# Encoder layer with PEER experts, one core: two builds' transposes stand ahead of blocks of U, and the loop's first G is loaded in the middle of the last build

## The chip, the cores and the metric

The kernel runs on one core of a Trainium2 chip. The metric is the device time of one execution in microseconds (us). The time before is the median of three runs, 1491.64 us (1488.11 to 1492.6). The profile shows one execution of its own, and durations are taken from that one.

Engine names: PE does the matrix products (PEld loads its weights), DVE the elementwise work on vectors, ACT the activations and copies, POOL issues the indirect DMAs (gathers), SP issues most plain DMAs; ACT issues DMAs too, in its own instruction stream.

## The reference

One encoder layer over 512 tokens of width 1024. The last part is the one that matters here:

```
h   = LN1(alpha * h + concat(a_na, a_mla) @ W_o)
q   = h @ w_q                        # 8 heads, two halves of 128
v1,i1 = top16(q[:half] @ sub_keys[0]);  v2,i2 = top16(q[half:] @ sub_keys[1])
cv,ci = top16(v1[:,None] + v2[None,:])          # 16 of 16384 experts per head
e1,e2 = i1[ci // 16], i2[ci % 16];  idx = e1 * 128 + e2;  g = softmax(cv)
ffn = sum_e  g_e * gelu(h . u_table[idx_e]) * v_table[idx_e]      # 128 experts per token
h   = LN2(alpha * h + ffn + sigmoid(h @ W_g + b_g) * (p @ W_ple))
```

## The kernel before

The 512 tokens are four chunks of 128. For chunk 0 the experts' rows are gathered from DRAM (POOL) and reduced on DVE. For chunks 1 to 3 the experts are computed densely: for each of 128 blocks of 128 experts, `ge = gelu(U_block . h)`, times a weight matrix `G` (tokens by experts, mostly zero), times the block of V. For chunk 1 (`NGC`) the 128 own rows of U are gathered too (`own_rows`), and their result stands in `G` in place of the softmax weight, so for this chunk `ge` is not needed.

Before the dense loop, `G` is built, one chunk at a time: first chunk 2, then chunk 3, then chunk 1. They are called chunk 2's, chunk 3's and the last build below. `build_g` starts with three transposes on PE (`tr` from e1, e2 and the weights, L1090), from which DVE and ACT make `eT` (L1098 to L1104). Then come 16 steps `q` of eight tokens: DVE and ACT write one-hots (`oh_i`, `oh_j`, L1144 to L1156), PE multiplies them 16 times into `tr` (L1115), ACT copies that to a staging tile `g_st` (L1128). Each four steps fill one staging tile, of which `send` writes four parts to DRAM, one per call; `send` is an instruction of ACT. Two tiles are used in turn, so the third group of a build waits for the writes of the first. The last two groups of the last build stay on the chip. The loop's first eight rows of G come from one load, `first_g` (tile `gt1`, L1447), of the two earlier builds' share; the last build copies its own share in on ACT (L1132).

PE has other work to put in between: the products of blocks of U with chunks 2 and 3, called blocks below (`lead_block`, L1291, eight products each, tiles `mm` and `hp`). 108 of the 128 blocks are done before the loop. Their loads (`raw`, `raw_u`, and at first borrowed tiles) are issued by SP as tiles come free, at most four in the ring.

The order on each engine is written by hand: the code runs inside `tc.manual_schedule`, so what is written first stands first. `run_pe(amount)` emits blocks of U on PE until a planned debt `due` is paid; `run(steps, share)` walks a build's steps and lets `own` (the gathers and reductions of rows on DVE) take a share beside them. After the own rows of chunk 1, `beside()` does the first 26 gathered rows of chunk 0 in the same way, and cuts two blocks of V near its end.

Every DMA that SP or ACT issues takes one of eight semaphores in turn, and waits for the transfer that used it last.

Of the kernel before, what the change touches and what calls it, by code (L numbers as in the profile page):

```python
# [9 lines left out]
F32 = mybir.dt.float32  # L10
# [21 lines left out]
N_S = 128  # L32
N_U = N_D - N_S
GT = 32
G_PARTS = 4
GB = 8
LEAD = 108
SPILL = 96
# [2 lines left out]
FIRST = 40  # L41
PACE = 1.1
AHEAD = 14.0
LAG = 6.0
BESIDE = 26
PRE = BESIDE
OWN = 1.2
OWN_G = 0.7
OWN_G_LATE = 4.0
SEAM = 7.0  # L50
WAIT = 8.4
OWN_LATE = 10.0
LATE = 0.57
OT = 8
# [25 lines left out]
def tile_encoder_layer(ctx: ExitStack, tc: tile.TileContext, A: dict, out: bass.AP):  # L80
    nc = tc.nc
# [8 lines left out]
    dram = ctx.enter_context(tc.tile_pool(name="dram", bufs=1, space=bass.MemoryType.DRAM))  # L90
# [205 lines left out]
    with tc.tile_pool(name="ln0", bufs=1, reuse_waits="tile") as ln0, \  # L296
# [122 lines left out]
        parts = turn(0)  # L419
# [17 lines left out]
        parts = turn(1)  # L437
# [8 lines left out]
        parts = turn(2)  # L446
# [8 lines left out]
        parts = turn(3)  # L455
# [374 lines left out]
    NGC, NDC = N_G // 128, N_D // 128  # L830
    NTG = N_D // GT
    u_rows, v_rows = A["u_rows"], A["v_rows"]
    ge_dram = dram.tile([SPILL, 128, N_U], F32, name="ge_dram")
    g_dram = dram.tile([NTG, 128, 128 * GT], F32, name="g_dram")

    pB = ctx.enter_context(tc.tile_pool(name="pB", bufs=1, reuse_waits="tile"))
    base = [pB.tile([128, D], F32, name=f"base_{c}") if c < NGC else h[c] for c in range(4)]
# [104 lines left out]
    for g in range(16):  # L942
# [8 lines left out]
        if g:  # L951
            i, t = next(homes)
# [113 lines left out]
    parts = []  # L1066

    def send():

        if parts:  # L1070
            g, t, x = parts.pop(0)
            n = 128 // G_PARTS
            nc.scalar.dma_start(g_dram[g][:, x * n * GT:(x + 1) * n * GT],
                                t[:, x * n:(x + 1) * n].rearrange("p i t -> p (i t)"))

    def run_pe(amount):
        nonlocal due
        due += amount * PACE
        while due > 0:
            done = next(pe_work, 1e9)  # L1080
            due -= done
        if due < -1e6:
            due = 0.0

    def build_g(c, e1, e2, gw):

        nonlocal due, nst
        ps = ps_tile("tr")
        for i, x in enumerate((e1, e2, gw)):
            nc.tensor.transpose(ps[:, i * 128:(i + 1) * 128], x, ident)  # L1090
        due -= 0.35
        yield None
        e32 = bt.tile([128, 3, 128], F32, name="eT", bufs=1)
        ne = e32[:, 2]
        eT = e32[:, 0:2].rearrange("p a b -> p (a b)").bitcast(F16).rearrange("p (x g s t) -> p x g s t", x=2, s=2, t=OT)
        keys, wt = eT[:, 0], eT[:, 1]
        pairs = bt.tile([128, 128, 2], F16, name="ne", bufs=1)
        nc.vector.tensor_copy(keys.rearrange("p g s t -> p s g t"),  # L1098
                              ps[:, 0:256].rearrange("p (s g t) -> p s g t", s=2, t=OT))
        w = ps[:, 256:384].rearrange("p (g t) -> p g t", t=OT)  # L1100
        nc.scalar.mul(wt[:, :, 0], w, W_SCALE)
        nc.scalar.mul(ne, ps[:, 0:128], -1.0)
        nc.vector.tensor_copy(pairs, iota.unsqueeze(2).to_broadcast([128, 128, 2]))
        nc.vector.scalar_tensor_tensor(wt[:, :, 1], w, W_SCALE, wt[:, :, 0], op0=OP.mult, op1=OP.subtract)  # L1104
        yield 1.2
        np_ = OT // 2

        def products(q, oh, oj):
            out = []
            for r in range(OT // 4):  # L1110
                ps = ps_tile("tr")
                for i in range(4):
                    a, b = divmod(4 * r + i, 2)
                    for part in range(2):
                        nc.tensor.matmul(ps[:, i * 128:(i + 1) * 128], oj[:, part, a, :, b], oh[:, a, :, b],  # L1115
                                         start=(part == 0), stop=(part == 1))
                out.append(ps)
            return out

        def leave(q, sums):  # L1120
            nonlocal stage, nst
            if q * OT % GT == 0:
                gone(f"bs{nst % 2}")
                stage = bs[nst % 2].tile([128, 128, GT], F32, name="g_st")
                nst += 1
            for r, ps in enumerate(sums):
                x = OT * q % GT + 4 * r
                nc.scalar.mul(stage[:, :, x:x + 4], ps.rearrange("p (t i) -> p i t", t=4), 1.0 / W_SCALE)  # L1128
            if (q + 1) * OT % GT == 0:
                g = (c - NGC) * (128 // GT) + q * OT // GT  # L1130
                if c == NGC:
                    nc.scalar.copy(first_g[:, g], stage[:, SPILL:SPILL + GB, :])  # L1132
                if c == NGC and g >= N_S // GT - 2:
                    g_last.append(stage)
                else:
                    parts.extend((g, stage, x) for x in range(G_PARTS))

        stage = None
        ahead = None
        wide = [128, 2 * np_, 128, 2]  # L1140
        for q in range(128 // OT):
            oh = bt.tile(wide, F16, name="oh_i")
            by_v = [128, 2 * np_ - OI_ACT, 128, 2]
            nc.vector.tensor_tensor(oh[:, OI_ACT:], pairs.unsqueeze(1).to_broadcast(by_v),  # L1144
                                    keys[:, q].rearrange("p s (a b) -> p (s a) b", b=2)[:, OI_ACT:].unsqueeze(2)
                                    .to_broadcast(by_v), op=OP.is_equal)
            for i in range(2 * OI_ACT):
                nc.scalar.activation(oh[:, i // 2, :, i % 2], iota, AF.Abs, bias=ne[:, OT * q + i:OT * q + i + 1])
            nc.scalar.activation(oh[:, 0:OI_ACT], oh[:, 0:OI_ACT], AF.Relu, bias=1.0, scale=-1.0)
            if ahead:  # L1150
                sums = products(*ahead)
                due -= G_SPLIT
            yield SPLIT_OH
            oj = bt.tile([128, 2, np_, 128, 2], F16, name="oh_j")
            for part in range(2):
                nc.vector.tensor_tensor(oj[:, part], oh[:, np_:],  # L1156
                                        wt[:, q, part].rearrange("p (a b) -> p a b", b=2).unsqueeze(2)
                                        .to_broadcast([128, np_, 128, 2]), op=OP.mult)
                if part == 0:
                    yield SPLIT_OJ  # L1160
            if ahead:
                leave(ahead[0], sums)
            ahead = (q, oh, oj)
            yield SPLIT_OJ
        sums = products(*ahead)
        due -= G_SPLIT
        yield 0.3
        leave(ahead[0], sums)
# [250 lines left out]
    with tc.manual_schedule(engines={nc.vector.engine, nc.scalar.engine, nc.tensor.engine, nc.sync.engine,  # L1419
                                     nc.gpsimd.engine}):  # L1420
        fill()
        held = []
        run(route(NGC, held))
        own = own_rows(*held)
        run_pe(next(own))
        own_due = -OWN_LATE
        for c in range(NGC + 1, 4):
            res = []
            if c > NGC + 1:
                run(route(0, []), OWN)  # L1430
            run(route(c, res), OWN)
            if c > NGC + 1:
                run_pe(WAIT)
            run(build_g(c, *res), OWN)
        own_due = 1e9
        run([0.0], 1.0)
        side = beside()
        run_pe(next(side))
        for _ in own:
            pass  # L1440
        own = None
        run_pe(LAG)

        while parts:
            send()
        first_g = pX.tile([128, NTG, GB, GT], F32, name="gt1")
        nc.sync.dma_start(first_g[:, 128 // GT:].rearrange("p g i t -> p g (i t)"),  # L1447
                          g_dram[128 // GT:, :, SPILL * GT:(SPILL + GB) * GT].rearrange("g p x -> p g x"))
        build = build_g(NGC, *held)
        next(build)  # L1450
        run_pe(next(side))
        own = side
        own_due = -OWN_G_LATE
        run(build, OWN_G)
        for x in own:
            run_pe(x)
        while parts:
            send()
        pb.close()
# [3 lines left out]
    def load_g(n, q, t, opens):  # L1463

        i = order[n]
        if opens:
            if n // GB % 2 == 0:
                t = pX.tile([128, NTG, GB, GT], F32, name="gt1")
            else:
                t = pV.tile([128, NTG, GB, GT], F32, name="gt0")  # L1470
        g = slice(q * NTG // 4 + (q == 1), (q + 1) * NTG // 4 - (q == 0))
        if q < 2:
            nc.scalar.copy(t[:, N_S // GT - 2 + q], g_last[q][:, i:i + GB, :])
        nc.sync.dma_start(t[:, g].rearrange("p g i t -> p g (i t)"),
                          g_dram[g, :, i * GT:(i + GB) * GT].rearrange("g p x -> p g x"))
        return t

    def block_of_u(n):
# [84 lines left out]
    with tc.manual_schedule(engines={nc.vector.engine, nc.sync.engine}):  # L1563
        for n, i in enumerate(order):
# [38 lines left out]
            parts = [t.rearrange("p (g t) -> p g t", t=GT) for t in (ah, al)] + [a]  # L1603
            if n in v_cut:
                held_a.append([t[:, :N_S // GT] for t in parts])
                parts = [t[:, N_S // GT:] for t in parts]
# [131 lines left out]
```

## Time and profile before

| what | value |
|---|---|
| median of three runs | 1491.64 us |
| profiled execution, its own time | 1489.54 us |
| its span, first to last instruction | 1487.8 us |
| PE busy in the span | 1450.2 us, 97% |
| DVE busy | 1268.5 us, 85% |
| chunk 3's build | 712 to 803 us |
| last build | 803 to 880 us |
| dense loop on PE | 893 to 1477 us |

Times in views are from the span's start. A timeline row has start, duration, engine, line and operation; in brackets stands the idle time before it and what ended that. "x16" is a number of records; an f32 product of the program (blocks of U) leaves two records, an f16 one leaves one.

### The profile page before, as it was taken

The numbers are of one execution on the slowest core, as the hardware profiler recorded it, in microseconds if no ns is written. First come the engines' busy times: TensorE is split into PE (matmuls) and PEld (weight loads), VectorE is DVE, ScalarE is ACT, GpSimd is POOL, SyncE is SP. The second block draws the span as 40 slices with busy tenths as digits, with TensorE's granted clock in tenths as the row PEclk, the third lists the DMA queues.
The fourth block names the chain that finished last, engine by engine and source line by source line (L and its number), as shares of the span: only waits on it lengthen the run. The fifth ranks groups of instructions, "written<-read, shape, count | busy, mean of one in ns | idle before, by whom it ended". The sixth has DMA issues, their size and how long they took to land.

```text
span 1487.8 us, 22518 instructions
## 1 busy us (share of the span) xinstructions
PE 1450.2 (97%) x7693; PEld 1212.4 (81%) x7693; DVE 1268.5 (85%) x2736; ACT 638.4 (43%) x1203; POOL 570.7 (38%) x520
## 2 busy tenths in 40 slices
PE   9999999999999999999998999999999999999997
PEld 5788777788888878888887888988888888888775
DVE  7376786579998979998776987999899999999997
ACT  3355776243221554212555763444343333333433
POOL 1013110010014544344442435665555666666630
PEclk9999999999999999999999999999999999999999
DMA  7333340175239999999999999999999999999992
GB/s 255 99 111 92 97 128 30 29 245 170 100 125 351 334 416 415 405 324 336 392 416 410 376 396 369 415 417 417 401 393 411 412 412 411 412 412 412 411 362 85
DMA packets 196851, 453.82 MB, mean 305 GB/s; under 512 B 18945, under 2 KB 96897, under 8 KB 196738
## 3 DMA queue, kind: packets, MB, share of 16 engines
q1 hardware_dynamic: 119168, 211.72, 38.6%
q0 software_dynamic: 57984, 207.12, 35.5%
q10 hardware_dynamic: 19586, 33.57, 5.9%
q8 instruction: 60, 0.98, 0.2%
q14 instruction: 53, 0.43, 0.1%
HBM read 411.70 MB, written 37.75 MB: 302 GB/s over the span
## 4 chain that ended last, share of the span: by engine, by line
PE 56%; DMA 22%; DVE 9%; issue 6%; ACT 4%; POOL 3%; SPq 0%; ACTq 0%; DVEq 0%; POOLq 0%
PE acc L1551 16%; DMA raw<-in_v_rows_dram 11%; PE mm L1291 6%; PE hp L1291 5%; DMA ge_dram<-ge 4%; PE mm L129 4%; PE mm L131 4%; PE mm L130 4%; PE pj L129 3%; PE pj L130 3%; PE pj L131 3%; DMA v_raw<-in_v_rows_dram 3%; PE hp L129 1%; PE hp L131 1%; PE hp L130 1%
## 5 line engine op out<-in xcount | busy, mean ns | idle before, releaser
L110 DVE TENSOR_TENSOR wlo<-raw,whi 128x1024 fp32r<-128x1024 f32 (+4 forms) x113 | 131.5, 1164 | 45.7 <-ACT whi L110 45.4
L110 ACT CAST a_hi<-gt 128x384 fp32r<-128x384 f32 (+2 forms) x128 | 64.9, 509 | 242.4 <-DVE gt L1598 179.5
L110 ACT CAST whi<-raw 128x1024 fp32r<-128x1024 f32 (+4 forms) x113 | 113.0, 1001 | 106.9 <-PE mm L130 47.3
L1291 PE MATMUL mm<-whole,raw 128*128 128x256 f32 x672 | 153.1, 381 | 1.5 <-DMA raw<-in_uT_dram 1.5
L1174 POOL DMA_INDIRECT whi<-in_u_rows_dram,s_ix x51 | 64.2, 1259 | 218.5 <-DVE cand L994 129.7
L1551 PE MATMUL acc<-hTh,a_hi 128*128 128x512 f32 x456 | 141.8, 391 | 0.1
L1551 PE MATMUL acc<-hTl,a_hi 128*128 128x512 f32 x456 | 141.2, 390 | 0.0
L1551 PE MATMUL acc<-hTh,a_lo 128*128 128x512 f32 x456 | 140.9, 389 | 0.0
L1291 PEld LDWEIGHTS mm<-whole,raw 128*128 128x128 f32 x672 | 125.6, 190 | 17.9 <-DMA raw<-in_uT_dram 1.9
L1534 POOL DMA_INDIRECT gat<-in_v_rows_dram,i_sel x64 | 100.8, 1574 | 55.0 <-DVE base L1536 39.5
L110 ACT CAST hTh<-v_raw 128x1024 fp32r<-128x1024 f32 x74 | 77.8, 1051 | 55.9 <-PE acc L1551 23.1
L1551 PEld LDWEIGHTS acc<-hTl,a_hi 128*128 128x128 f32 x456 | 85.4, 188 | 18.3 <-DVE hTl L110 0.4
L1551 PEld LDWEIGHTS acc<-hTh,a_lo 128*128 128x128 f32 x456 | 85.4, 188 | 18.2 <-DVE a_lo L110 0.3
L1551 PEld LDWEIGHTS acc<-hTh,a_hi 128*128 128x128 f32 x456 | 84.1, 188 | 17.2 <-ACT a_hi L110 1.1
L110 DVE TENSOR_TENSOR hTl<-v_raw,hTh 128x1024 fp32r<-128x1024 f32 x74 | 90.2, 1219 | 6.4 <-ACT hTh L110 6.4
L1551 PE MATMUL acc<-wlo,a_hi 128*128 128x512 f32 x300 | 92.8, 390 | 0.2
L1551 PE MATMUL acc<-whi,a_hi 128*128 128x512 f32 x300 | 92.8, 391 | 0.1
L1551 PE MATMUL acc<-whi,a_lo 128*128 128x512 f32 x300 | 92.6, 390 | 0.0
L1174 POOL DMA_INDIRECT wlo<-in_u_rows_dram,s_ix x51 | 61.9, 1213 | 68.3 <-DVE s_dot L1176 56.0
L1519 POOL DMA_INDIRECT gat<-in_u_rows_dram,i_sel x52 | 69.1, 1329 | 45.2 <-DVE hdot L1525 34.1
L1536 DVE SCALAR_TENSOR_TENSOR base<-gat,hdot,base 128x1024 f32<-128x1024 f32 x64 | 82.0, 1281 | 1.0
L1273 ACT ACTIVATE ge<-mm 128x256 f32<-128x256 f32 x78 | 29.6, 380 | 110.4 <-PE mm L1291 100.5
(415 smaller groups left out, 3815.7 us busy)
## 6 DMA issues: line engine op xcount, KB each, us to landing
raw<-in_uT_dram SPq DMA_DIRECT2D x80, 512.0 KB, 7.8
v_raw<-in_v_rows_dram SPq DMA_DIRECT2D x78, 512.0 KB, 13.2
raw<-in_v_rows_dram SPq DMA_DIRECT2D x48, 512.0 KB, 13.8
g_dram<-g_st ACTq DMA_DIRECT2D x40, 512.0 KB, 12.1
ge_dram<-ge ACTq DMA_DIRECT2D x96, 128.0 KB, 7.0
ge<-ge_dram SPq DMA_DIRECT2D x96, 128.0 KB, 13.0
gt<-g_dram SPq DMA_DIRECT2D x30, 384.0 KB, 13.9
raw_u<-in_uT_dram SPq DMA_DIRECT2D x19, 512.0 KB, 7.8
```

Of the source, the lines that this page charges most:

```text
L110: cut = nc.scalar.copy(hi, src), nc.vector.tensor_tensor(lo, src, r32(hi), op=OP.subtract)
L129: nc.tensor.matmul(ps, a[0], b[0], start=start, stop=False)
L130: nc.tensor.matmul(ps, a[0], b[1], start=False, stop=False)
L131: nc.tensor.matmul(ps, a[1], b[0], start=False, stop=stop)
L1174: nc.gpsimd.indirect_dma_start(out=u[:], out_offset=None, in_=u_rows, in_offset=bass.IndirectOffsetOnAxis(ap=ix[:, k:k + 1], axis=0))
L1273: nc.scalar.activation(ge, ps[:, :N_U], AF.Gelu)
L1291: nc.tensor.matmul(ps[:, :N_U], raw[:, k], whole[:, k, :], start=(k == 0), stop=(k == 7))
L1519: nc.gpsimd.indirect_dma_start(out=u[:], out_offset=None, in_=u_rows, in_offset=bass.IndirectOffsetOnAxis(ap=i_sel[:, c, k:k + 1], axis=0))
L1534: nc.gpsimd.indirect_dma_start(out=u[:], out_offset=None, in_=v_rows, in_offset=bass.IndirectOffsetOnAxis(ap=i_sel[:, c, k:k + 1], axis=0))
L1536: nc.vector.scalar_tensor_tensor(base[c], u, hdot[:, c, k:k + 1], base[c], op0=OP.mult, op1=OP.add)
L1551: nc.tensor.matmul(acc[c][hf], a[:, cs], b[:, hf * 512:(hf + 1) * 512], start=(n == 0 and i == 0), stop=(n == 127 and i == 2))
```

## The change

Four edits:

1. `WAIT` 8.4 to 3.0 and `LAG` 6.0 to 1.0: fewer blocks of U are emitted ahead of the transposes of chunk 3's build and of the last build.
2. After the last build's transposes, `GAP_ROWS` = 4 gathered rows of chunk 0 stand on DVE before the build goes on, where one stood.
3. The three last parts of chunk 3's G are no longer sent in one go ahead of the last build; the sends go on one by one. `first_g` is loaded when step q = 6 of the last build is written.
4. The last build's first two groups are written to a DRAM tensor of their own, `g_own`.

```diff
-LAG = 6.0
+LAG = 1.0
-WAIT = 8.4
+WAIT = 3.0
+FIRST_G_AT = 6
+GAP_ROWS = 4
...
-    g_dram = dram.tile([NTG, 128, 128 * GT], F32, name="g_dram")
+    g_own = dram.tile([N_S // GT - 2, 128, 128 * GT], F32, name="g_own")
+    g_dram = dram.tile([NTG - N_S // GT, 128, 128 * GT], F32, name="g_dram")
...
-            nc.scalar.dma_start(g_dram[g][:, x * n * GT:(x + 1) * n * GT],
+            to = g_own[g] if g < N_S // GT else g_dram[g - N_S // GT]
+            nc.scalar.dma_start(to[:, x * n * GT:(x + 1) * n * GT],
...
+    def load_first():
+        while parts and parts[0][0] >= N_S // GT:
+            send()
+        nc.sync.dma_start(first_g[:, N_S // GT:].rearrange("p g i t -> p g (i t)"),
+                          g_dram[:, :, SPILL * GT:(SPILL + GB) * GT].rearrange("g p x -> p g x"))
...
+            if c == NGC and q == FIRST_G_AT:
+                load_first()
...
         run_pe(LAG)
-        while parts:
-            send()
         first_g = pX.tile([128, NTG, GB, GT], F32, name="gt1")
-        nc.sync.dma_start(first_g[:, 128 // GT:].rearrange("p g i t -> p g (i t)"),
-                          g_dram[128 // GT:, :, SPILL * GT:(SPILL + GB) * GT].rearrange("g p x -> p g x"))
         build = build_g(NGC, *held)
         next(build)
-        run_pe(next(side))
+        for _ in range(GAP_ROWS):
+            run_pe(next(side))
         own = side
```

How instructions move. On PE, at the start of chunk 3's build, the order before is (`tr<-ident` are the transposes, the last row the build's first product):

```order
L1291 MATMUL mm<-whole,raw 128x256 x24
L1090 MATMUL tr<-ident,e_6432 128x128
L1090 MATMUL tr<-ident,e_6599 128x128
L1090 MATMUL tr<-ident,gw 128x128
L1291 MATMUL mm<-whole,raw_u 128x256 x8
L1291 MATMUL mm<-whole,raw 128x256 x18
L1115 LDWEIGHTS oh_j
L1115 MATMUL tr<-oh_i,oh_j 128x128
```

and with the change, at the same place:

```order
L1304 MATMUL mm<-whole,raw 128x256 x10
L1101 MATMUL tr<-ident,e_6433 128x128
L1101 MATMUL tr<-ident,e_6600 128x128
L1101 MATMUL tr<-ident,gw 128x128
L1304 MATMUL mm<-whole,raw 128x256 x14
L1304 MATMUL mm<-whole,raw_u 128x256 x8
L1304 MATMUL mm<-whole,raw 128x256 x4
L1126 LDWEIGHTS oh_j
```

14 products of blocks of U moved from ahead of the transposes to later places; between the transposes and the first product 26 stand in both.

On PE, at the start of the last build (behind the last product of the build before it), the order before is:

```order
L1291 MATMUL mm<-whole,raw_u 128x256 x4
L1291 MATMUL mm<-whole,raw 128x256 x13
L1090 MATMUL tr<-ident,e1s 128x128
L1090 MATMUL tr<-ident,e2s 128x128
L1090 MATMUL tr<-ident,gws 128x128
L1291 MATMUL mm<-whole,raw 128x256 x11
L1115 LDWEIGHTS oh_j
```

and with the change:

```order
L1304 MATMUL mm<-whole,raw 128x256 x4
L1101 MATMUL tr<-ident,e1s 128x128
L1101 MATMUL tr<-ident,e2s 128x128
L1101 MATMUL tr<-ident,gws 128x128
L1304 MATMUL mm<-whole,raw 128x256 x5
L1304 MATMUL mm<-whole,raw_u 128x256 x8
L1304 MATMUL mm<-whole,raw 128x256 x6
L1126 LDWEIGHTS oh_j
```

Ahead of the transposes 17 products became 4, behind them 11 became 19. What is left over goes to the end: behind the last build's last product and ahead of the loop's first `acc` stand 50 products of blocks of U instead of 33.

On ACT, at the same place, the order before is (the DMA rows are the sends of G and of `ge`):

```order
L1273 ACTIVATE ge<-mm 128x256
L1275 DMA ge_dram<-ge 128x256
L1073 DMA g_dram<-g_st 128x1024 x3
L1101 ACTIVATE eT<-tr 128x16x8
L1102 ACTIVATE eT<-tr 128x128
L1148 ACTIVATE oh_i<-iota,eT 128x128 x4
L1149 ACTIVATE oh_i<-oh_i 128x512
```

and with the change:

```order
L1286 ACTIVATE ge<-mm 128x256
L1288 DMA ge_dram<-ge 128x256
L1112 ACTIVATE eT<-tr 128x16x8
L1113 ACTIVATE eT<-tr 128x128
L1077 DMA g_dram<-g_st 128x1024
L1159 ACTIVATE oh_i<-iota,eT 128x128 x4
L1160 ACTIVATE oh_i<-oh_i 128x512
L1077 DMA g_dram<-g_st 128x1024 x2
```

The three sends moved from ahead of `eT` to behind it, one ahead of the first one-hot and two behind it. On SP the load of `first_g` (`gt<-g_dram`, 128x8x256) moved back past four loads of blocks of U, with fewer loads left between it and the loads of V. On DVE three more gathered rows (`row`, `whi`, `wlo`) stand ahead of `eT`; the first cut of a block of V (`hTl<-gb`) stands ahead of the last step's `oh_j` instead of behind it, and so does ACT's half of it ahead of the last copies to `g_st`.

More of the change, by code (lines that the diff above doesn't have):

```diff
@@ L1474, in load_g @@
         nc.sync.dma_start(t[:, g].rearrange("p g i t -> p g (i t)"),
-                          g_dram[g, :, i * GT:(i + GB) * GT].rearrange("g p x -> p g x"))
+                          (g_dram[g.start - N_S // GT:g.stop - N_S // GT] if q else g_own)
+                          [:, :, i * GT:(i + GB) * GT].rearrange("g p x -> p g x"))
         return t
```

## The prediction

> **What bounds the kernel now.** I read the busy times of the page first, then windows of the stages that the change touches, then who waited for whom, then the timeline at the two places where transposes stand.
>
> ```profile
> PE 1450.2 (97%) x7693; PEld 1212.4 (81%) x7693; DVE 1268.5 (85%) x2736; ACT 638.4 (43%) x1203; POOL 570.7 (38%) x520
> ```
>
> PE is busy 97% of the span, and the change adds and removes no product. So it can gain only idle time of PE, and it can lose only by new idle time. The next rows are windows: length, busy us of PE, PEld, DVE, ACT and POOL, then the granted clock, the DMA share and GB/s. They are chunk 3's build, the last build with the blocks behind it, the loop, and ten us inside the last build.
>
> ```profile
> 700.00:803.00 103.00, 99.82 (x646) 87.55 (x645) 79.97 (x132) 55.79 (x138) 45.63 (x39) 1.00 1.02 407
> 803.00:893.30 90.30, 84.62 (x571) 74.07 (x569) 70.59 (x113) 59.62 (x148) 28.49 (x24) 0.98 0.99 389
> 893.30:1443.00 549.70, 549.37 (x2641) 461.82 (x2640) 522.49 (x700) 213.73 (x307) 333.03 (x226) 1.00 1.03 407
> 860.00:870.00 10.00, 8.28 (x60) 7.28 (x58) 9.96 (x15) 8.65 (x23) 4.38 (x4) 0.83 1.03 418
> ```
>
> PE is idle 3.18 us in chunk 3's build, 5.68 in the last one, 0.33 in the loop. So what is at stake is 8.9 us, 0.6% of the time. The waits of PE (total, times, longest) say for what, the first two rows in chunk 3's build, the other four in the last:
>
> ```profile
> PE tr L1115 <- ACT g_st L1128: 2.3, 3, 1.5
> PE tr L1115 <- DVE oh_j L1156: 0.9, 1, 0.9
> ...
> PE tr L1115 <- ACT g_st L1128: 2.8, 2, 1.7
> PE mm L1291 <- DMA raw<-in_uT_dram: 1.5, 1, 1.5
> PE tr L1115 <- ACT oh_i L1149: 1.1, 1, 1.1
> PE tr L1115 <- DVE oh_j L1156: 0.3, 1, 0.3
> ```
>
> PE waits for ACT and DVE, though DVE itself stands still at the start of both builds. The timeline:
>
> ```profile
> 701.43 10.52 PE L1291 MATMUL mm<-whole,raw 128*128 128x256 f32 x48
> 711.79 0.38 PE L1090 MATMUL tr<-ident,e 128*128 128x128 f32 x2
> 712.32 0.42 DVE L1098 CAST eT<-tr 128x256 f16<-128x256 f32 x1 [5.90 <-PE tr L1090]
> ...
> 800.94 1.22 DVE L1176 CUSTOM_DVE_ANT_0 wlo<-wlo,h 128x1024 f32<-128x1024 f32 x1
> 802.36 1.94 PE L1291 MATMUL mm<-whole,raw_u 128*128 128x256 f32 x8
> 804.14 5.78 PE L1291 MATMUL mm<-whole,raw 128*128 128x256 f32 x26
> 809.97 0.27 PE L1090 MATMUL tr<-ident,gws 128*128 128x128 f32 x1
> 810.35 0.42 DVE L1098 CAST eT<-tr 128x256 f16<-128x256 f32 x1 [8.18 <-PE tr L1090]
> 811.29 2.24 ACTq L1073 DMA_DIRECT2D g_dram<-g_st  x3
> 813.58 0.28 ACT L1101 ACTIVATE eT<-tr 128x128 f16<-128x128 f32 x1 [5.41 <-DMA ge_dram<-ge]
> 814.06 0.29 DVE L1104 SCALAR_TENSOR_TENSOR eT<-tr,eT 128x128 f16<-128x128 f32 x1 [3.09 <-ACT eT L1102]
> 816.08 0.22 PE L1115 MATMUL tr<-oh_i,oh_j 128*128 128x128 f16 x1 [1.09 <-ACT oh_i L1149]
> ```
>
> The transposes stand behind blocks of U, and DVE loses 5.90 us in the one build and 8.18 + 3.09 in the other; the 3.09 are ACT's, which makes its half of `eT` only after three sends of G.
>
> **The change part by part.** The sum is made against the profiled execution, 1489.54 us with a span of 1487.8; that is 2.1 us under the median of the runs, 1491.64, and the same difference is taken off the median.
>
> *Chunk 3's transposes.* 48 records are 24 products and take 10.36 us to the next start, 0.432 each. 14 of them less put the transposes 6.0 us earlier, which takes away DVE's 5.90. PE reaches the first product 6.0 us earlier too, since 26 products stand behind the transposes as before. So PE, DVE and ACT run this build in the same relation, some 6 us earlier; no gain yet, since the 14 products are only owed. Its 3.18 us of idle I keep: the sends and the DMA rate that hold ACT are the same. Ends: all 3.2 gained, or as much lost again.
>
> *Last build's start.* Its transposes now stand 4 products (1.7 us) behind 802.36, so at 804.2 on the old scale. DVE first does three more rows, whose gathers POOL issued here; the median from issue to landing between 740 and 803 us is in the next rows:
>
> ```profile
> 793.32 1.16 POOL L1174 DMA_INDIRECT row<-in_u_rows_dram,i_sel  x1 [5.37 <-DVE s_dot L1176]
> 796.25 1.03 POOL L1174 DMA_INDIRECT wlo<-in_u_rows_dram,i_sel  x1 [0.30 <-issue]
> ...
> g_dram<-g_st ACTq DMA_DIRECT2D x12, 512.0 KB, 14.2
> raw<-in_uT_dram SPq DMA_DIRECT2D x10, 512.0 KB, 7.7
> wlo<-in_u_rows_dram,s_ix POOLq DMA_INDIRECT x6, 12.6
> row<-in_u_rows_dram,s_ix POOLq DMA_INDIRECT x4, 11.2
> ```
>
> The rows land at 804.5 to 808.9, so DVE ends the third at about 809 to 810 and reads the transposes hardly earlier than at 810.35. It has done 3 x 1.22 = 3.7 us of rows by then, and ACT's sends no longer stand ahead of `eT` (3.1): DVE is about 7 us ahead of its old place, on top of the 6. PE comes to its first product after 4 + 19 products, at 802.4 + 9.9 + 0.5 = 812.8; DVE needs 0.3 + 0.95 + 1.3 us behind `eT`, so 812.5 to 813.5. The old wait of 1.39 shrinks to about 0.4: **gain 1.0** (ends: 1.4 gained; 3 lost, if a send held ACT as long as before, 3.09).
>
> *The load of first_g.* SP sat on it for 11.5 us, until chunk 3's last part of G was written, and PE then missed a block of U:
>
> ```profile
> SPq L1447 <- DMA g_dram<-g_st: 11.5, 1, 11.5
> ...
> 827.99 1.56 PE L1291 MATMUL mm<-whole,raw 128*128 128x256 f32 x6 [1.46 <-DMA raw<-in_uT_dram]
> ```
>
> At q = 6, some 22 us into the 16 steps (814 to 873 us, rows above and below), those writes, 14.2 us long, have landed, and the writes of the last build go to `g_own`, for which the load doesn't wait. In the queue it stands between loads of U for blocks not yet due. **Gain 1.4** (0 to 1.46).
>
> *The middle of the last build.* The remaining two gaps, 1.11 and 1.72, and a product group slow at a granted clock of 0.83 (window 860 to 870 above):
>
> ```profile
> 853.59 1.09 ACT L1128 ACTIVATE g_st<-tr 128x512 f32<-128x512 f32 x2 [2.09 <-DMA g_dram<-g_st]
> 855.94 1.08 PE L1115 MATMUL tr<-oh_i,oh_j 128*128 128x128 f16 x16
> 859.04 1.11 PE L1115 MATMUL tr<-oh_i,oh_j 128*128 128x128 f16 x16 [1.11 <-ACT g_st L1128]
> 861.87 1.86 PE L1115 MATMUL tr<-oh_i,oh_j 128*128 128x128 f16 x16 [1.72 <-ACT g_st L1128]
> ```
>
> 16 products took 1.86 us instead of 1.08, so these two gaps cost 2.83 + 0.78 = 3.6. ACT was late because the third staging tile waited 2.09 us for the writes of the first. Those writes keep their length, and an earlier DVE doesn't shorten them: I take a third, **gain 1.2** (0 to 3.6). By the Trainium skill, page "TensorE: Matmul & The Clock Gate", section "Why this matters for your kernels", the array falls back only after a gap of some 3 us; the trace disagrees with that bound, with 1.72 and the slow group behind it, and by the page alone the ceiling of this term would be 2.8.
>
> *Costs put at nothing.* ACT's and DVE's halves of the first cut of V now stand inside the build's end, about 1.2 us each. DVE had its last `oh_j` done 3.7 us before PE used it and is now further ahead:
>
> ```profile
> 873.29 1.28 DVE L1156 TENSOR_TENSOR oh_j<-oh_i,eT 128x1024 f16<-128x1024 f16 x2
> 878.27 1.08 PE L1115 MATMUL tr<-oh_i,oh_j 128*128 128x128 f16 x16
> 886.58 7.07 PE L1291 MATMUL hp<-whole,raw 128*128 128x256 f32 x32
> ```
>
> The 17 products owed (7.3 us) stand ahead of the loop; they are no new work. Their four or five loads need 7.7 us each with four tiles in the ring, and a block takes 8 x 0.432 = 3.5 us, so the ring covers 13.8; without that cover a late load costs up to 4 us once. The loop's own order is unchanged, apart from `g_own`'s name.
>
> Sum: 1.0 + 1.4 + 1.2 = 3.6 us earlier at the loop's first `acc`, which was at 893.3. In the loop PE is idle 0.33 us in 550, so I let the end move as far: 1489.5 becomes 1485.9, the median 1491.6 becomes **1488.0**.
>
> **The rivals.**
>
> *All idle goes.* DVE and ACT come so early that the gaps of both builds vanish: 3.2 + 5.7 + 0.8 = 9.7 us at most, and half of chunk 3's and all of the last build's is 8: 1482 to 1486. For it: nearly all gaps are waits for ACT or DVE, which gain 13 us of lead, while PE gives up 7.3 of its own. Against it: ACT's waits on writes of G.
>
> *The loop eats it.* The loop runs at 407 GB/s with a DMA share of 1.03, and no row shown is above 418; DVE is busy 522 of 550. If its DMA stream is the true limit, PE starts earlier and later waits for V, and the end stays: 1491.6, give or take 1.5. Against it: PE kept its full pace with 0.33 us of idle, and the same transfers start earlier as well. The Trainium skill, page "DMA: Bandwidth & Descriptors", section "Where 436 GB/s comes from", puts the ceiling of the ports at 435; the trace's 407 to 418 lie near it, which speaks for this rival.
>
> *Slower: ACT's sends wait for their semaphores.* Now a send stands between `eT` and the first one-hot, and two behind it. Each waits for the transfer that had its semaphore before, which takes up to 14.2 us from issue by the row of G's writes. ACT may be late by about 1 us before PE is; beyond that PE waits one for one. To end 4.5 us above, the waits must come to 3.6 + 4.5 + 1 = 9 us: 1496 to 1500. Against it: the same three sends cost ACT 5.41 together before.
>
> **How the numbers follow.** Changes under 0.3%, 4.5 us, can't be told from none here. Chances: partial gain 0.40 (1485.5 to 1490, of which 0.14 lies beyond 4.5 us), all idle gone 0.24, eaten by the loop 0.22, slower 0.14. So faster 0.24 + 0.14 = 0.38, within 0.3% 0.26 + 0.22 = 0.48, slower 0.14. The likeliest case's own range is 1485.5 to 1490; the range to hold 8 in 10 reaches from the second case's lower part, 1483, to 1494.5, above the third, and leaves the slower case out.
>
> **What would show it.** Right: `eT` of chunk 3 at about 706 with a DVE wait under 1 us; no wait of SP for G's writes at `first_g`; PE idle in the last build under 4 us; 50 products in one stretch ahead of `acc`, whose first starts near 890. Wrong: an ACT wait above 3 us at the sends behind the last `eT`; DVE waiting for gathers in the gap longer than 8 us; PE waiting for `raw` in the last stretch; or `acc` at 890 with new waits for V from 1340 us on.

## The result, and the profile after

The changed kernel takes 1500.97 us (median of 6 runs, 1496.91 to 1502.6), the kernel before 1488.42 in the same job: a ratio of 1.007 [1.0057, 1.0084]. It is 12.5 us slower, where 3.6 us less were forecast. (Three of the six runs of the kernel before are the ones of the prediction, with their median of 1491.64; the three others have one of 1487.89.)

The profiled execution took 1501.62 us, its span is 1499.5. First PE's line of the page, then windows as in the prediction (length, busy us of PE, PEld, DVE, ACT, POOL, clock, DMA share, GB/s): chunk 3's build, from there to the loop's first `acc`, the loop over the same 549.7 us, and ten us in the middle of the last build.

```profile
PE 1452.0 (97%) x7693; PEld 1214.3 (81%) x7693; DVE 1270.0 (85%) x2736; ACT 638.8 (43%) x1203; POOL 575.9 (38%) x520
...
700.00:803.00 103.00, 99.35 (x639) 87.02 (x638) 83.15 (x135) 56.24 (x139) 48.34 (x40) 0.98 1.03 410
803.00:905.10 102.10, 86.64 (x569) 76.11 (x567) 67.82 (x109) 59.71 (x146) 26.37 (x21) 0.92 0.90 341
905.10:1454.80 549.70, 548.90 (x2642) 462.09 (x2640) 522.86 (x700) 213.13 (x307) 336.10 (x226) 1.00 1.03 406
...
850.00:860.00 10.00, 3.87 (x21) 3.45 (x21) 2.88 (x5) 6.03 (x15) 1.15 (x1) 0.50 1.03 420
```

The first `acc` starts at 905.1 instead of 893.3, 11.8 us later. PE is idle 15.5 us between 803 and that point, where it was 5.7; the loop itself has 0.8 of idle. So the loss arises before the loop. Who PE waited for between 700 and 905 us:

```profile
PE tr L1126 <- ACT g_st L1139: 16.5, 3, 11.7
PE tr L1126 <- DVE oh_j L1169: 2.6, 2, 2.4
```

The waits at which the change aimed are gone. In the timeline, `eT` of chunk 3 comes at 704.27 (before 712.32), that of the last build at 803.14 (before 810.35), and DVE stands idle ahead of neither:

```profile
704.27 0.42 DVE L1109 CAST eT<-tr 128x256 f16<-128x256 f32 x1
...
803.14 0.42 DVE L1109 CAST eT<-tr 128x256 f16<-128x256 f32 x1
803.60 0.33 ACTq L1077 DMA_DIRECT2D g_dram<-g_st  x1
804.07 0.29 DVE L1115 SCALAR_TENSOR_TENSOR eT<-tr,eT 128x128 f16<-128x128 f32 x1 [0.26 <-ACT eT L1113]
```

There are two new costs. The first is one gap of 11.65 us on PE. The rows are those of SP's issue of first_g's load, of ACT's instructions around its send nine microseconds late, and of PE; the last row gives the load's time from issue to landing.

```profile
832.90 0.43 SPq L1084 DMA_DIRECT2D gt<-g_dram  x1
...
843.77 0.41 ACT L1143 COPY gt<-g_st 128x256 f32<-128x256 f32 x1
852.79 0.33 ACTq L1077 DMA_DIRECT2D g_own<-g_st  x1
853.16 1.31 ACT L1159 ACTIVATE oh_i<-iota,eT 128x128 f16<-128x128 f32 x4 [8.98 <-DMA gt<-g_dram]
...
843.40 1.08 PE L1126 MATMUL tr<-oh_i,oh_j 128*128 128x128 f16 x16
856.13 1.87 PE L1126 MATMUL tr<-oh_i,oh_j 128*128 128x128 f16 x16 [11.65 <-ACT g_st L1139]
...
gt<-g_dram SPq DMA_DIRECT2D x1, 1024.0 KB, 19.9
```

ACT's send at 852.79 had, by the program's order, the same semaphore as first_g's load, eight DMAs of SP and ACT earlier, and was issued only when that load had landed (832.90 + 19.9 = 852.8). The load took 19.9 us (5.6 before). ACT stood 8.98 us, with the one-hots and the copies of the next groups queued behind the send, and PE 11.65.

The second cost is at the end of the last build: its last product, the 50 products of blocks behind it, the loop.

```profile
882.71 1.08 PE L1126 MATMUL tr<-oh_i,oh_j 128*128 128x128 f16 x16
883.63 4.53 PE L1304 MATMUL mm<-whole,raw 128*128 128x256 f32 x20
888.00 3.62 PE L1304 MATMUL hp<-whole,raw 128*128 128x256 f32 x16
891.45 3.62 PE L1304 MATMUL hp<-whole,raw_u 128*128 128x256 f32 x16
894.91 10.52 PE L1304 MATMUL hp<-whole,raw 128*128 128x256 f32 x48
905.08 0.80 PE L1562 MATMUL acc<-hTh,a_hi 128*128 128x512 f32 x2
```

The builds started 7 to 8 us earlier, and the last product came 4.4 us *later* (before 878.27). So the 17 products that the change moved behind it were not paid for by an earlier end; they lie bare.

### The profile page after: what moved, and what is told of

The parts are those of the page before. It is cut to its first block, busy times and chain, and to the rows that moved or that the text cites. A ratio compares the mean times of both kernels' runs of the same rounds, so it can differ in the third digit from the quotient of the medians.

```text
span 1499.5 us, 22521 instructions
## 1 busy us (share of the span) xinstructions
PE 1452.0 (97%) x7693; PEld 1214.3 (81%) x7693; DVE 1270.0 (85%) x2736; ACT 638.8 (43%) x1203; POOL 575.9 (38%) x520
## 4 chain that ended last, share of the span: by engine, by line
PE 55%; DVE 12%; DMA 11%; issue 11%; POOL 7%; ACT 3%; SPq 0%; ACTq 0%; POOLq 0%; DVEq 0%
PE acc L1562 24%; PE mm L131 3%; PE mm L132 3%; PE mm L133 3%; DMA raw<-in_v_rows_dram 3%; POOL whi L1187 3%; PE pj L131 3%; POOL wlo L1187 3%; PE pj L132 3%; PE mm L1304 3%; PE pj L133 3%; PE hp L1304 2%; DMA v_raw<-in_v_rows_dram 2%; PE hp L131 1%; PE hp L133 1%
## 5 line engine op out<-in xcount | busy, mean ns | idle before, releaser
L1304 PEld LDWEIGHTS mm<-whole,raw 128*128 128x128 f32 x640 | 121.0, 193 | 15.6
L112 DVE TENSOR_TENSOR a_lo<-gt,a_hi 128x384 fp32r<-128x384 f32 (+2 forms) x128 | 69.7, 546 | 21.6 <-ACT a_hi L112 21.0
## 6 DMA issues: line engine op xcount, KB each, us to landing
gt<-g_dram SPq DMA_DIRECT2D x30, 384.0 KB, 14.1
```

Of the source, the lines that this page charges most:

```text
L112: cut = nc.scalar.copy(hi, src), nc.vector.tensor_tensor(lo, src, r32(hi), op=OP.subtract)
L1304: nc.tensor.matmul(ps[:, :N_U], raw[:, k], whole[:, k, :], start=(k == 0), stop=(k == 7))
```

## The experiments

Two stretches split every run's time. A is from the first product of all builds to the last one's start, B from there to the loop's first `acc`. Their ends are the start times in group rows like these, of before:

```profile
L1115 PE MATMUL tr<-oh_i,oh_j x768: 217/218/308, 491.3 to 879.1; 128*128 128x128 f16 x192
L1551 PE MATMUL acc<-hTh,a_hi x456: 388/389/580, 893.3 to 1476.7; 128*128 128x512 f32 x152
```

A is 879.1 - 491.3 = 387.8, B 893.3 - 879.1 = 14.2. From the first to the last start of `acc` are 581.3 to 584.1 us in all runs, so the rest of the time hardly moves. "Behind" is the number of products of blocks behind the last build's last product.

| run | median, us | before, same job | ratio | A | behind | B |
|---|---|---|---|---|---|---|
| before | 1488.4 | | | 387.8 | 33 | 14.2 |
| after | 1501.0 | 1488.4 | 1.0070 [1.0057, 1.0084] | 392.3 | 50 | 21.5 |
| e1_pool | 1495.7 | 1489.4 | 1.0044 [1.0027, 1.0060] | 385.9 | 50 | 21.5 |
| e2_q8 | 1496.5 | 1489.4 | 1.0051 [1.0034, 1.0069] | 387.8 | 50 | 21.5 |
| e3_load_only | 1493.2 | 1489.4 | 1.0032 [1.0019, 1.0045] | 390.2 | 33 | 14.2 |
| e4_starts | 1500.6 | 1489.4 | 1.0068 [1.0052, 1.0085] | 386.0 | 59 | 25.4 |
| e5_fill_last | 1499.9 | 1489.3 | 1.0070 [1.0050, 1.0090] | 401.1 | 33 | 14.1 |
| e6_fill_both | 1504.9 | 1489.3 | 1.0094 [1.0065, 1.0124] | 406.4 | 18 | 7.7 |
| e7_half_rows_before | 1475.7 | 1489.3 | 0.9912 [0.9887, 0.9938] | 372.3 | 33 | 14.2 |
| e8_half_rows_q8 | 1478.1 | 1489.3 | 0.9922 [0.9902, 0.9942] | 368.8 | 50 | 21.5 |
| e9_pool8 | 1494.8 | 1489.5 | 1.0034 [1.0014, 1.0054] | 388.2 | 50 | 21.5 |
| e10_pool8_fill_last | 1491.2 | 1489.5 | 1.0008 [0.9993, 1.0022] | 394.7 | 33 | 14.2 |
| e11_pool8_fill_both | 1493.8 | 1489.5 | 1.0037 [1.0019, 1.0056] | 396.5 | 18 | 7.7 |
| e12_load_pool8 | 1488.1 | 1489.5 | 0.9990 [0.9976, 1.0004] | 387.2 | 33 | 14.2 |
| e13_last_early | 1495.9 | 1488.9 | 1.0054 [1.0037, 1.0071] | 387.4 | 45 | 19.3 |
| e14_chunk3_early | 1495.3 | 1488.9 | 1.0045 [1.0031, 1.0058] | 388.3 | 46 | 19.8 |
| e15_gap_rows | 1490.9 | 1488.9 | 1.0016 [1.0007, 1.0026] | 391.8 | 24 | 10.3 |
| e16_last_early_gap | 1493.7 | 1488.9 | 1.0029 [1.0017, 1.0042] | 393.7 | 36 | 15.4 |

A and B are of the one profiled execution; that of e10 was 5.5 us above its run's median, that of e9 2.9 above, that of e15 3.2 below, the others within 2.1. B is 0.43 us per product in every row: (21.5 - 14.2) / 17 = 0.429. The loss of `after` is 4.5 in A and 7.3 in B, 11.8 together.

**The load's semaphore: another queue, or two groups later.**

```diff
e1_pool, in load_first:
-        nc.sync.dma_start(first_g[...
+        nc.gpsimd.dma_start(first_g[...
e2_q8:
-FIRST_G_AT = 6
+FIRST_G_AT = 8
```

> The changed kernel with first_g's load issued by POOL at the same step q = 6, so that it takes none of the eight semaphores that SP's and ACT's transfers share; same bytes, same time. Theory S (the semaphore): ACT's first send of the second own group no longer waits 9.0 us for first_g's load, PE's gap of 11.65 us falls under 3, the loop's first acc comes some 9 us before 905, time 1489 to 1493. Theory B (the bytes): a load of 1 MB in 1 KB pieces among full queues holds up gathers, writes and loads of U whatever its semaphore; the gap stays near 11, time 1498 to 1502. Theory T (staging): the third staging tile waits for g_own's writes; the gap stays above 8, ACT's wait being named g_own.

> The changed kernel with FIRST_G_AT 8 instead of 6: the load stands four transfers later in the program, and the next user of its semaphore is a load of a block of U on SP instead of a send of ACT. Theory S: ACT's 9.0 us wait is gone, SP may wait some us instead; time 1489 to 1493. Theory B: the load lands as late, 15 to 20 us, and the gap moves two steps later, 8 to 12 us; time 1498 to 1502. Theory T as in the changed kernel, 1498 to 1502.

They measured 1495.7 and 1496.5, 5.2 and 4.5 us less than `after`, both above theory S's range of 1489 to 1493: it had the wait right and thought it worth more. In both the 11.65 is gone, and the largest gaps of PE are 2.6 and 3.6 us. In e2 the next DMA on the load's semaphore is one of SP's, and SP waits 11.0 us there without harm. So the semaphore is the first cause, worth about 5 us; 6 to 7 remain, and A is back at its old length. POOL's load had a wait of its own in e1, with the gathers queued behind it:

```profile
827.36 0.96 POOL L1084 DMA_DIRECT2D gt<-g_dram  x1 [10.16 <-DMA ge_dram<-ge]
```

**Parts of the change on the kernel before.** e3_load_only has edits 3 and 4, e4_starts edit 1.

```diff
e3_load_only, from after:
-LAG = 1.0
-WAIT = 3.0
-GAP_ROWS = 4
+LAG = 6.0
+WAIT = 8.4
+GAP_ROWS = 1
e4_starts, from before:
-LAG = 6.0
-WAIT = 8.4
+LAG = 1.0
+WAIT = 3.0
```

> The kernel before with edits 3 and 4 alone (first_g at q = 6, its own tensor, sends one by one; LAG 6.0, WAIT 8.4 and one row in the gap as before). The next user of the load's semaphore is again a send of ACT (the third of the second group). Theory S: SP's wait of 11.5 us goes, but that send waits for the load, 3 to 9 us later than it would; PE loses 2 to 9 us there and has 6 us more of blocks in hand; time 1489 to 1498. Theory E (the early transposes are the cost): 1486 to 1489.

> The kernel before with edit 1 alone (LAG 1.0, WAIT 3.0; the load and the three sends ahead of the last build as before). Theory S: no long wait at a send in the middle of the last build; the last build starts some 6 us earlier, but ACT still has three sends ahead of eT; time 1486 to 1490. Theory E (PE runs out of blocks between products once 14 of them are moved to the end): gaps of 5 us and more in both builds, time 1495 to 1501.

e3 (1493.2) lies in theory S's range and e4 (1500.6) in theory E's, but E expected gaps of 5 us and more in both builds, and e4 has one such gap in all, described below. The early transposes alone cost 11.2 us, nearly as much as the whole change (12.5): A is 1.8 shorter, but 59 products lie behind it, B is 25.4. And the load, which e4 still has at the build's head, now held SP 13.0 us at a worse moment: PE missed a block for 9.72 us (1.46 before).

```profile
827.15 1.22 PE L1291 MATMUL mm<-whole,raw 128*128 128x256 f32 x2 [9.72 <-DMA raw<-in_uT_dram]
```

The moved load alone cost 3.9 us. Its reader, an addition on DVE to first_g's tile, stood ready at 842 us, long before the load had landed at 853. A send of ACT waited 7.2 us for the load, as theory S said, and PE waited 4.5 us for a block of U, issued behind the load, that landed late too:

```profile
853.29 0.42 DVE L1609 TENSOR_TENSOR gt<-gt,g_raw 128x256 f32<-128x256 f32 x1 [10.93 <-DMA gt<-g_dram]
...
854.47 2.93 PE L1304 MATMUL mm<-whole,raw_u 128*128 128x256 f32 x6 [4.52 <-DMA raw_u<-in_uT_dram]
```

**Putting the moved products back into the builds.** Theory D, in the form in which the rest tests it: the builds end when the DMA queues let them, so an earlier start ends nothing earlier, and moved products are added. If the idle time in the builds can take the products again, the loss goes.

```diff
from e2_q8, in run(): (extra 0 elsewhere)
-            run_pe(amount)
+            run_pe(amount + extra)
e5_fill_last: extra = 0.14 in the last build
e6_fill_both: and 0.115 in chunk 3's
```

> The changed kernel with first_g's load at group 8 (as in e2_q8, 1496.5 us) and 0.14 more of PE work taken at each step of the last build, so that 33 products of blocks stay behind its last product, as many as before the change, instead of 50. Theory D (the two builds end when the DMA queues have brought their rows, so earlier transposes end nothing earlier, and every product moved behind the last one is added bare): the last product stays at 879 to 882 us of the span, the loop starts 7 us earlier than in e2_q8, at 894 to 897, and the time is 1488.5 to 1491. Rival P (PE is the bound in the last build too, and what is put back only moves the last product later by the same 17 x 0.43 = 7.3 us): last product at 887, time 1495 to 1497.5.

> As e5_fill_last, with 0.115 more of PE work at each step of chunk 3's build as well: 18 products stay behind the last build's last one. Theory D, if the queues alone bound both builds: PE's idle time in the builds (12.8 us in e2_q8) takes the 32 products (13.8 us), last product at 879 to 883, loop start 888 to 891, time 1482.5 to 1486. Theory D with PE as the second bound: PE had 8.9 us of idle time left in this stretch before the change, and its products are the same, so no more than about 5 us of it can be gained: 1485 to 1490. Rival P: the last product later by 13.8 us, 893, time 1495 to 1497.5.

Both missed theory D's numbers: 1499.9 and 1504.9. The blocks done earlier brought the addition to first_g's tile forward to 852 and 859 us, where the load had not landed; DVE waited 11.2 and 11.0 us for it. So these two do not decide on D; they show that the load must also have landed when its reader comes.

```profile
863.22 0.43 DVE L1615 TENSOR_TENSOR gt<-gt,g_raw 128x256 f32<-128x256 f32 x1 [11.24 <-DMA gt<-g_dram]
```

**Fewer gathers.**

```diff
e7_half_rows_before, e8_half_rows_q8, in rows():
+            if k % 2 == 0:
+                j = k // 2
                 u = ...tile(... names by j)
                 nc.gpsimd.indirect_dma_start(out=u[:], ...
```

> The kernel before with only every second of the 128 gathers of rows of U issued for its own scores; the other row's products are taken from the same tile, so 64 gathers of a [128, D] tile are left out and DVE's work is the same. Theory D: the stretch of chunk 3's build is bound by the queues, which lose about 64 x 0.5 MB here: DVE's 13.4 us of waits for gathers go, and with the eT waits (5.90, 8.18) then the longest ones, the last product comes 3 to 8 us earlier: 1481 to 1486. Rival P (PE and DVE bound the builds, and the gathers' waits lie beside PE's work): within 2 us of 1489.

> e2_q8 with the same 64 gathers left out. Theory D: now the earlier transposes can be used: the waits for gathers that took the place of the eT waits (20.5 us on DVE in e2_q8) shrink, and the last product comes at 870 to 875 instead of 880, so that against e7_half_rows_before the loss of 7 us shrinks to 0 to 4 us: 1482 to 1488. Rival P: the last product no earlier than in e2_q8 by over 1 us, and 7 us over e7_half_rows_before, 1495 to 1497.

The edit leaves out more than the expectation says: 64 of 128 gathers of own rows and 13 of the 26 of chunk 0's rows. The groups' starts, e7 first (`eT` of chunk 3 and of the last build, then the products):

```profile
L1098 DVE CAST eT<-tr x2: 424/424/425, 707.7 to 802.1; 128x256 f16<-128x256 f32 x2
L1115 PE MATMUL tr<-oh_i,oh_j x768: 217/218/233, 493.6 to 865.9; 128*128 128x128 f16 x192
```

```profile
L1109 DVE CAST eT<-tr x2: 417/421/425, 701.4 to 792.6; 128x256 f16<-128x256 f32 x2
L1126 PE MATMUL tr<-oh_i,oh_j x768: 217/218/308, 493.4 to 862.2; 128*128 128x128 f16 x192
```

Both runs came in below all the ranges (1475.7 and 1478.1). The kernel before gets 13.6 us faster with half the gathers, so the gathers held its builds, though PE was 95% busy there. Two things went together here: the DMA share from 700 us to the last product fell from 1.01 to 0.92, and DVE's waits for gathered rows (13.4 us in chunk 3's build) are gone. The run doesn't separate them, and of the 15.5 us by which A shrinks only 5.0 lie behind the last build's `eT`. With the gathers halved, a start 9.5 us earlier ends the last build 3.7 us earlier, and the change (with its load at group 8) costs 2.4 us instead of the 7.1 of e2. That is what D says in direction. PE is the next bound: its idle time from 700 to 893 us is 2.3 us in e7 and 4.8 in e8, and 3.60 of the latter are one wait for ACT.

**The load out of the way.** Four gathers later on POOL's queue the load itself waited 0 to 4.2 us, not 10.2. e9 is the change so; e10 and e11 are e9 with the products put back as in e5 and e6; e12 has only the load moved.

```diff
e9_pool8, from after:
-FIRST_G_AT = 6
+FIRST_G_AT = 8
-        nc.sync.dma_start(first_g[...
+        nc.gpsimd.dma_start(first_g[...
e12_load_pool8, from e9:
-LAG = 1.0
-WAIT = 3.0
-GAP_ROWS = 4
+LAG = 6.0
+WAIT = 8.4
+GAP_ROWS = 1
```

> The changed kernel with first_g's load on POOL's queue at group 8: four gathers later on that queue than in e1_pool, where the load's own wait held POOL for 10.2 us, and away from the semaphores of SP and ACT. It is the base for e10 and e11, and lies without the load's waits: 50 products of blocks behind the last build's last one, as in the changed kernel. Theory D (what is left of the loss is idle time of PE: the products moved behind the build are missing in it as filling): PE's idle time in 700 us to the loop 11 to 14 us, loop start 899 to 902, time 1492.5 to 1495.5. Rival F (all of the loss is the late load): no wait for the load, so loop start at 893 to 895, time 1486.5 to 1489.5.

> e9_pool8 with 0.14 more of PE work at each step of the last build, so 33 products stay behind it, as before the change. In e5_fill_last, the same with the load on SP, DVE waited 11.2 us for the load (it adds to first_g's tile at 852 us there) and PE 9.4 and 1.5 us for DVE. Theory D: with the load landed by then those 10.9 us go, loop start 893 to 897, 1487 to 1490.5, that is 4 to 7 us less than e9. Rival P (PE is the bound in the last build, what is put back only moves its end): as e9 or slower, 1493 to 1497.

> e10 with 0.115 more at each step of chunk 3's build too, 18 products behind the last build. Theory D: the idle time of chunk 3's build (about 3 us) can be filled as well: 1484 to 1489. Rival P: 1496 to 1500, more than e10 by the 6.5 us that are moved.

> The kernel before with only the load moved and the tensor of its own (e3_load_only), but the load on POOL's queue at group 8; transposes and blocks as before the change. In e3 DVE waited 10.9 us for the load, and PE 4.5 us behind it. Theory L (the moved load is worth what its SP wait cost, and loses it by landing late at its reader): both waits go, loop start 890 to 893, 1485 to 1488.5. Rival: another wait takes its place, 1491 to 1494 as in e3.

e12 came at 1488.1, as theory L said: without its waits the moved load costs nothing and, at 0.9990 [0.9976, 1.0004], gains nothing that can be told. e9 (1494.8, in D's range) is 6.7 us above it. So edits 1 and 2 cost that by themselves, and rival F is out. e10 gets 3.6 of it back, a little less than D's 4 to 7; e11 came at 1493.8, between the two theories' ranges and above e10. The gaps in both moved to ACT's sends at 852 to 857 us (PE waits of 6.8 and 7.9 us). A doesn't tell more here: by it the products put back in e10 lengthen the builds by 6.5 of their 7.3 us, as rival P says, but that profile is the slowest of its ten runs.

**The edits one by one, on e12.**

```diff
from e12_load_pool8:
e13, e16:  -LAG = 6.0     +LAG = 1.0
e14:       -WAIT = 8.4    +WAIT = 3.0
e15, e16:  -GAP_ROWS = 1  +GAP_ROWS = 4
```

> e12_load_pool8 (1488.1 us, 33 products of blocks behind the last build) with one more edit of the change: the last build's transposes 5 us of PE work earlier. 45 products stay behind. Theory D (the last product's time is set by the queues and the chain of groups, not by when the build starts): 12 products x 0.43 = 5.2 us more, 1491.5 to 1494.5. Rival P (PE is the bound, so products that move behind the build are no new work): 1486.5 to 1489.5.

> e12_load_pool8 with the transposes of chunk 3's build 5.4 us of PE work earlier, nothing else. 46 products stay behind the last build. Theory D: 13 x 0.43 = 5.6 us more, 1492 to 1495. Rival P: 1486.5 to 1489.5.

> e12_load_pool8 with four pieces of the side work ahead of the last build's first group instead of one, transposes as before the change. 24 products stay behind, 9 fewer. Theory D: up to 9 x 0.43 = 3.9 us less if the last product stays in its place, 1484 to 1487; the edit is then the one that gains. Rival P: the last product moves later by what is put ahead of it, 1487 to 1490.

> e13 and e15 together on e12_load_pool8: 36 products stay behind. Theory D: 3 x 0.43 = 1.3 us more than e12, 1488 to 1491. Rival P: 1486.5 to 1489.5. The two lie close here; the run is for the sum of the parts and as a candidate for a faster kernel.

e13 against e12 is the cleanest pair. `eT` of both builds, the products and the loop, e12 first:

```profile
L1109 DVE CAST eT<-tr x2: 425/425/425, 713.9 to 812.2; 128x256 f16<-128x256 f32 x2
L1126 PE MATMUL tr<-oh_i,oh_j x768: 217/218/308, 493.2 to 880.4; 128*128 128x128 f16 x192
L1562 PE MATMUL acc<-hTh,a_hi x456: 389/389/580, 894.6 to 1476.6; 128*128 128x512 f32 x152
```

```profile
L1109 DVE CAST eT<-tr x2: 424/424/424, 714.0 to 806.3; 128x256 f16<-128x256 f32 x2
L1126 PE MATMUL tr<-oh_i,oh_j x768: 217/218/314, 493.2 to 880.6; 128*128 128x128 f16 x192
L1562 PE MATMUL acc<-hTh,a_hi x456: 387/389/582, 899.9 to 1481.5; 128*128 128x512 f32 x152
```

The last build's `eT` comes 5.9 us earlier, its last product at the same time, and the loop 5.3 us later, for 12 products at 0.43. The lead went in waits like this one of ACT, behind sends of G (in e12 its longest there is 3.3), and in what followed on PE. The rows are ACT's, PE's behind it, and the window from 803 us to the last product, of e12 and of e13:

```profile
856.92 0.60 ACT L1139 ACTIVATE g_st<-tr 128x512 f32<-128x512 f32 x1 [6.19 <-DMA ge_dram<-ge]
857.57 1.86 PE L1126 MATMUL tr<-oh_i,oh_j 128*128 128x128 f16 x16 [4.65 <-ACT g_st L1139]
...
803.00:880.40 77.40, 71.61 (x521) 63.25 (x521) 60.30 (x96) 53.74 (x136) 29.43 (x25) 0.98 1.00 390
803.00:880.60 77.60, 69.80 (x497) 60.73 (x497) 60.82 (x98) 53.13 (x133) 29.18 (x24) 0.93 0.99 379
```

PE's idle time grows by only 2.0 us, from 5.8 to 7.8. The granted clock falls from 0.98 to 0.93, and 24 records fewer (12 products, 5.2 us) take only 1.8 us off PE's busy time. So about 3.4 us, an estimate from these rows, are the same work at a lower clock: what a gap costs is more than its length.

By the medians e13 costs 7.8 us against e12 and e14 7.2 (against each job's own kernel before it is 0.6 more), both above D's 5.2 and 5.6; the profiled executions of e12 and e13 differ by 5.0, and the rest of the 7.8 has no cause shown. Rival P, for which moved products are no new work, is refuted by both. In e14 the lead of chunk 3's build lasts to the last build's `eT` (804.3) and is lost behind it, too.

e15 missed D. Nine products fewer lie behind, B is 3.9 shorter, but A is 4.6 longer; the median is 2.8 above e12, just above P's range. It did not start later: the last build's first product comes at 816.23 (816.73 in e12). It lost its time in one gap, at the same place as in e13, where ACT waited for the writes of `g_own`:

```profile
854.01 0.60 ACT L1139 ACTIVATE g_st<-tr 128x512 f32<-128x512 f32 x1 [4.76 <-DMA g_own<-g_st]
854.65 1.86 PE L1126 MATMUL tr<-oh_i,oh_j 128*128 128x128 f16 x16 [6.62 <-ACT g_st L1139]
```

e16 lies 5.5 above e12, beyond both ranges, with a gap of 7.70 us there. The parts do not add up: last build's start, chunk 3's and the rows cost 7.8, 7.2 and 2.8 us alone, and 6.7 together (e9). None of the sixteen runs beats the kernel before by more than can be told, apart from the two that leave gathers out.

What stays open is which transfers hold the last build: gathers, blocks of U and G's writes share the queues, and only the gathers were taken away. That full queues set its pace is argued, not shown: from 803 us to the last product the DMA share is 1.00 in e12 and 0.99 in e13, but 0.96 in e14 and in the changed kernel. The long gaps stand where ACT waits, at its sends or for a staging tile, until earlier transfers have landed; the change was not tried with more than eight semaphores or with a third staging tile.

## Why the prediction was wrong

- **Right:** DVE's waits for the transposes went (5.90 and 8.18 to nothing, 3.09 to 0.26), SP's 11.5 us at first_g and PE's 1.46 behind it too, and 50 products stand in a stretch ahead of `acc`. A shift of the loop's start did reach the end: 11.8 us there, 12.1 in the profiled executions' times. So "the loop eats it" was rightly no case; its DMA share of 1.03 did not make it absorb a shift. Nor did it in the other direction: in e7 the loop starts 13.2 us earlier than in the kernel before, and its last `acc` starts 13.6 earlier.
- **The step that failed** is "The 17 products owed (7.3 us) stand ahead of the loop; they are no new work". They are no new work, but the sum took for granted that the last product would come at least as much earlier. That would hold where PE alone sets the pace. With half the gathers it holds by half: e8's last product comes 3.7 us earlier than e7's, for 7.3 us of products moved. In the last build as it is, it does not hold: e13 and e14 show 12 and 13 products (5.2 and 5.6 us) moved and A no shorter, 0.2 and 1.1 us longer; the lead went in ACT's waits for writes, PE's gaps behind them and the lower clock after the gaps. The rows that spoke against it were quoted: a DMA share of 1.02 at 407 GB/s in chunk 3's build and 418 GB/s in the window 860 to 870. I read the queues as a cause of single gaps, not as what could set the pace. PE's 95% hid it, since blocks of U fill any hole until none are left to fill with.
- **first_g's load** was given a gain of 1.4, bounded at nothing. Its cost was 4.5 to 5.2 us: I looked at what the load waits for and at what is queued behind it on SP, and not at who uses its semaphore next (an ACT send) nor at its reader on DVE. Its 5.6 us of before were no measure for the new place: there it took 19.9.
- **The last build's start** (1.0) and **its middle** (1.2) did not come: PE's idle time from 803 us on rose from 5.7 to 15.5.
- **The slower rival** had the mechanism, at 0.14 and 1496 to 1500: an ACT send held by its semaphore. It was not one of the three sends behind `eT` but one 49 us later, behind the load that the change itself had put there. That alone would have given some 1493 (1488.4 + 5, an estimate); the other 7 us no rival had. The 14.2 us that the prediction calls the most a transfer takes is a median; this one took 19.9.

## What to carry to other kernels

Work that fills holes of an engine is worth what the hole costs at its place: before moving it out of a stage, ask whether that stage ends earlier without it, and look at the DMA share there before the engine's busy share. A moved DMA has three due times, its source, its reader and the next user of its semaphore; list all three, with the landing time of the new place. And test the parts of a change alone: here the moved load was neutral once it was out of the way, either of the early starts cost some 7 us alone, and their fault was hidden behind the load's.

## What was not expected of the hardware

A 1 MB load took 19.9 us in the last build (17.3 to 17.9 in e5 and e6), with queues at 410 to 420 GB/s, against 5.6 us some 13 us earlier in the kernel before, so landing times are no property of a transfer. The short time fell into a lull of the queues. In the kernel before they moved 256 GB/s while the load ran, and almost nothing around its issue (17 GB/s from 819 to 821 us):

```profile
gt<-g_dram SPq DMA_DIRECT2D x1, 1024.0 KB, 5.6
...
819.80:825.40 5.60, 5.60 (x51) 4.98 (x50) 5.57 (x11) 4.73 (x14) 2.57 (x2) 1.00 0.82 256
```

Some groups of 16 products that follow a wait ran at a lower clock: 1.87 instead of 1.08 us behind the gap of 11.65, and a granted clock of 0.50 in the window 850 to 860. Shorter gaps differ. In e9:

```profile
843.59 1.87 PE L1126 MATMUL tr<-oh_i,oh_j 128*128 128x128 f16 x16 [2.42 <-ACT g_st L1139]
...
855.60 1.11 PE L1126 MATMUL tr<-oh_i,oh_j 128*128 128x128 f16 x16 [2.65 <-ACT g_st L1139]
```

The Trainium skill, page "TensorE: Matmul & The Clock Gate", section "Why this matters for your kernels", asks for no idle gaps above some 3 us between bursts. The gap of 11.65 agrees; the slow group behind 2.42 does not, and the one behind 2.65 ran at full pace, so the length of the last gap alone doesn't decide it here.
